# Output weights split on GpSimd alone, rows loaded ahead, and the decays' operations moved two steps behind their loads

## The chip, the cores and the metric

The kernel runs on one core of a Trainium2 chip. A core has a matrix engine (TensorE, PE in the profile), a vector engine (VectorE, DVE), an engine for functions of one input (ScalarE, ACT), a general one (GpSimd, POOL) and a sync engine whose queue issues most transfers (SyncE, SP). Each engine takes its instructions in the order in which they stand in its own queue; engines wait for each other through semaphores. The metric is the device time of one launch, in microseconds; the median over several runs is compared.

## The reference, cut to what matters

One layer of a streaming encoder runs for two groups of requests: a prompt of 2048 tokens and 8 streams with 16 new tokens each, 2176 tokens in all, 17 tiles of 128. A shared projection feeds two halves, a Mamba-2 state space mixer (SSD) and an attention with forget gates (FoX). Their results, concatenated, go through one output projection.

```python
def trunk(x, ...):
    n = rmsnorm(x, norm1_g[l])
    z, xbc, dt_raw, q, k, v, f_raw = split_columns(n @ w_in[l])
    y_ssd, ... = ssd_mixer(z, xbc, dt_raw, ...)
    y_fox = fox_prompt(q, k, v, logf)        # or fox_sample with the cache
    h = x + jnp.concatenate([y_ssd, y_fox], axis=-1) @ w_out[l]
    y_ffn, fc_new = conv_ffn(rmsnorm(h, norm2_g[l]), ...)
    x = h + y_ffn

def ssd_scan(xs, dt, a, bm, cm, s0):
    ...
    seg = a_cs[:, :, :, None, :] - a_cs[:, :, None, :, :]
    decay = jnp.exp(jnp.where(causal, seg, -jnp.inf))
    scores = jnp.einsum('bclhn,bcshn->bclsh', cc, bc) * decay
    y_diag = jnp.einsum('bclsh,bcshp->bclhp', scores, xdt)
    ...
```

## The kernel before

Tokens are worked in tiles of 128; the prompt's 16 tiles are numbered 0 to 15, the tile of the 8 streams is `SMP` (16). The prompt is also cut into four parts of 512 tokens. Up to about 1540 us the kernel interleaves three kinds of work on TensorE, and the order of TensorE's queue is written out by hand; behind that come the up- and down-projections (FFN). The order on the other engines and on SP's queue is set by a scheduler, which starts from program order and moves an instruction ahead or back by its own estimate of when its inputs are ready.

- **Attention** (`attention`, 320 steps). A step of `t_phase` computes one block of scores (`s<-q,k`, L728 and L729), its exponential on ScalarE (`pr<-s`, L733, kept in the list `exps`), and, two steps later, the product with the values (`pv<-pr,v`, L696). Beside it `s_phase` computes the maxima for a later head (`s<-ks,q`, L668; `nm`, L671). The tiles named `s` live in a PSUM pool of four buffers which attention and the state space chunks share, so TensorE can run only a few score blocks ahead of ScalarE's exponentials. Attention part p has 32(p+1) steps.
- **Side work** (`sides`). While a part of the attention runs, another generator is advanced in small units, evenly over the part's steps: the streams' attention in part 0, then the SSD chunks, one per tile (`ssd_chunk`). A chunk loads `xb` (convolved inputs, L525), `zt` (gate, L527) and `sg` (128x1024, the cumulated decays broadcast to all partitions, L529), each with one buffer. ScalarE turns `sg` into decays with eight Relu (L532, one per head) and one Exp over 1024 columns (L533). TensorE transposes and multiplies parts of `xb` (L536, L538), ScalarE copies one result to `bs` (L542), and further units use `sg` in the matmuls of L563, GpSimd's product `xe` (L557) in L573, and the state in L570. Every `yield` ends a unit, and the numbers in `sides` count them.
- **Fill** (`part_steps`, then `out_steps`): the input projections of the next part (`mm`, L397 to L399 and L444 to L446; `cmw` and `craw` are their weights) and, in the last part, the output projection. A tuple `("wait", n)` makes the fill pause for n attention steps.

`out_weights` prepares the output weights: eight tiles of 128x1024 are loaded (`raw`, two buffers, L896) and each is split into a rounded part and the rest (`wo`), because a product in full precision takes three matmuls of the fast type. ScalarE rounds (L109), GpSimd subtracts in two halves (L112), and `tc.issue_after(exps[-1])` keeps both behind the newest exponential. `out_proj(c)` loads the mixed rows of a tile (`raw<-mix_d`, L915, the same two buffers), splits them (`mx`, ScalarE L102 and VectorE L105), and runs 48 matmuls (`dn`, L923 to L925). Loads here stand on SP's queue. `load_v` clears half of a value tile on GpSimd (L636) before its load.

Of the kernel before, what the change touches and what calls it, by code (L numbers as in the profile page):

```python
# [11 lines left out]
AF = mybir.ActivationFunctionType  # L12
# [9 lines left out]
NB = 8  # L22
# [4 lines left out]
SMP = NTILE - 1  # L27
# [39 lines left out]
def hybrid_step(ctx: ExitStack, tc: tile.TileContext, i: dict, o: dict):  # L67
    nc = tc.nc
    V, S, G, T = nc.vector, nc.scalar, nc.gpsimd, nc.tensor
# [30 lines left out]
    def split(src, hi, lo, heng, leng):  # L100
        if heng is S:
            S.copy(hi, src)  # L102
        else:
            heng.tensor_copy(hi, src)
        leng.tensor_sub(lo, src, hi.bitcast(F32))  # L105

    def split2(src, hi, lo, leng):

        S.copy(hi, src)  # L109
        m = src.shape[1] // 2  # L110
        for c in (slice(0, m), slice(m, 2 * m)):
            leng.tensor_sub(lo[:, c], src[:, c], hi[:, c].bitcast(F32))  # L112
# [34 lines left out]
    def bt_(shape, tag, bufs, dt=F32):  # L147
        return bp.tile(shape, dt, tag=tag, name=tag, bufs=bufs)

    def pss():  # L150
        return psb.tile([P, 512], F32, tag="s", name="s", bufs=4)
# [370 lines left out]
    def ssd_chunk(c):  # L522
# [4 lines left out]
        dma(zt, z_d[c])  # L527
        sg = bt_([P, 8, P], "sg", 1)
        dma(sg.rearrange("p h l -> p (h l)"), ac_d[c:c + 1].rearrange("c h p -> c (h p)").to_broadcast([P, D]))  # L529

        for h in range(8):
            S.activation(sg[:, h], sg[:, h], AF.Relu, scale=-1.0, bias=acs[:, c, h:h + 1])  # L532
        S.activation(sg, sg, AF.Exp, scale=-1.0)  # L533
        pb = pss()
        for g in range(2):
            T.transpose(pb[:, g * P:(g + 1) * P], xb[:, 4 + g], ident)  # L536
# [156 lines left out]
    late, chores, exps = [], [], []  # L693
# [191 lines left out]


    tp = op = pso = None
    wo = []

    def out_weights():  # L890

        raws = {}

        def load(k):
            raws[k] = op.tile([P, D], F32, tag="raw", name="raw", bufs=2)
            dma(raws[k], i["w_out"][0, k * P:(k + 1) * P, :])  # L896

        load(0)
        load(1)
        yield ("wait", 3)  # L900
        for k in range(KT):
            w = op.tile([P, 2, D], F32R, tag="wo", name="wo", bufs=KT)
            with tc.issue_after(exps[-1]):
                split2(raws[k], w[:, 0], w[:, 1], G)
            wo.append(w)
            if k + 2 < KT:
                load(k + 2)
            yield ("wait", 2)

    def out_proj(c, after=None):  # L910
        mr = op.tile([P, KT, P], F32, tag="raw", name="raw", bufs=2)
        mx = op.tile([P, 2, KT, P], F32R, tag="mx", name="mx", bufs=2)

        for ks in ([slice(0, KT - 1), slice(KT - 1, KT)] if 12 <= c < 16 else [slice(0, KT)]):
            dA(mr[:, ks], mix_d[c][:, ks])  # L915
            split(mr[:, ks], mx[:, 0, ks], mx[:, 1, ks], S, V)
        y = op.tile([P, D], F32, tag="y", name="y", bufs=1)
        dA(y, i["xr"][c])
        ps = [pso.tile([P, 512], F32, tag="dn", name="dn") for _ in range(2)]

        def part(e, k):
            cc = slice(e * 512, (e + 1) * 512)
            T.matmul(ps[e], mx[:, 0, k], wo[k][:, 0, cc], start=k == 0, stop=False)  # L923
            T.matmul(ps[e], mx[:, 0, k], wo[k][:, 1, cc], start=False, stop=False)  # L924
            T.matmul(ps[e], mx[:, 1, k], wo[k][:, 0, cc], start=False, stop=k == KT - 1)  # L925

        with tc.issue_after(after) if after is not None else ExitStack():
            if c >= 12 and c != SMP:
                for k in range(KT):
                    for e in range(2):  # L930
                        part(e, k)
            else:
                for e in range(2):
                    for k in range(KT):
                        part(e, k)
                        if k % 2:
                            yield 1.36
        for e in range(2):
            cc = slice(e * 512, (e + 1) * 512)
            V.tensor_add(y[:, cc], y[:, cc], ps[e])  # L940
        dS(h_d[c], y)
# [190 lines left out]
    acs = cb.tile([P, NTILE, 8], F32, name="acs")  # L1132
# [31 lines left out]
    def chain(*gs):  # L1164
        for g in gs:
            yield from g

    def chunks(*cs):
        return chain(*(ssd_chunk(c) for c in cs))
# [28 lines left out]
    def out_steps():  # L1198
        A.close()
        open_out()  # L1200
        yield from out_weights()
        for c in [SMP] + list(range(11)):
            yield from out_proj(c)

    F = ExitStack()
    O = ExitStack()
# [1 line left out]
    def open_out():  # L1208
        nonlocal tp, op, pso
        tp = F.enter_context(tc.tile_pool(name="t3", bufs=2, reuse_waits="tile"))  # L1210
        op = O.enter_context(tc.tile_pool(name="op", bufs=1, reuse_waits="tile"))
        pso = O.enter_context(tc.tile_pool(name="pso", bufs=3, space=PSUM, reuse_waits="tile"))

    fill = [(0, 157.0, 20), (1, 140.0, 80), (2, 140.0, 172), (3, 69.0, 216), (4, 132.0, 318)]
    sides = {0: (sample_attention, 5 * NB + 1), 1: (lambda: chunks(SMP, 0, 1, 2), 49), 2: (lambda: chunks(3, 4, 5, 6, 7), 51),
             3: (lambda: chunks(*range(8, 16)), 81)}

    with tc.manual_schedule(engines={nc.tensor.engine}):
        bodies = [a_body(0)]
# [9 lines left out]
        n = hold = 0  # L1229
# [3 lines left out]
        for u in att:  # L1233
            if u is None:
                credit += 3.0
            else:
                if u != side_p:
                    for _ in side or ():
                        pass
                    side_p = u  # L1240
                    f, total = sides[u]
                    side, given, cnt = f(), 0, 0
                n += 1
                cnt += 1
                while given < total * cnt // (32 * (u + 1)):
                    next(side, None)
                    given += 1
                if hold:
                    hold -= 1
                    continue  # L1250
                if gen is not None:
                    start = fill[stage - 1][2] if stage else 0
                    credit += fill[stage][1] / (fill[stage][2] - start)
            while gen is not None and credit > 0 and not hold:
                c = next(gen, None)
                if c is None:
                    stage += 1
                    gen = (part_steps(stage) if stage < NPART else out_steps()) if stage < len(fill) else None
                elif isinstance(c, tuple):
                    hold = c[1]  # L1260
                else:
                    credit -= c
# [13 lines left out]
    for w, cs in zip(FPARTS[0], ((11, 12, 13), (14, 15))):  # L1276
        prep(w, True)
        for c in cs:

            for _ in out_proj(c, None if c >= 12 else pv_ins[-1]):  # L1280
                pass
# [109 lines left out]
```

## Time and profile before

| | us |
|---|---|
| median of 3 runs | 3158.28 (3156.93 to 3160.4) |
| the profiled execution's own time | 3159.18 |
| its span, from first to last instruction | 3157.5 |
| TensorE busy, with modelled ends | 3039.0 |
| VectorE, ScalarE, GpSimd busy | 1788.8, 1066.7, 865.8 |

Time lies in three stretches: up to about 460 us the first part's projections and the streams' attention, from 460 to 1540 us attention, chunks and fill together, and from there the FFN. What TensorE's idle time waited for stands behind an instruction in square brackets in the timeline: the idle time in us, and the releaser.

### The profile page before, as it was taken

The page shows a single profiled execution, that of the slowest core. Times are in us where ns is not written, and L with a number is a line of the kernel's source. Part 1 is how long each engine was busy: PE and PEld are TensorE (multiplying, and loading weights), DVE is VectorE, ACT ScalarE, POOL GpSimd, SP SyncE. Part 2 cuts the span into 40 slices and gives each one's busy share as a digit, 9 for nine tenths or more (in the row PEclk, how much of TensorE's full clock was granted, in tenths as well). Part 3 has the DMA queues.
Part 4 walks back from the last instruction along what each step waited for, and adds up shares of the span by engine and source line. Part 5 has one row for each costly group of instructions (what it writes and reads, how often), then busy time and mean ns, then how long its engine had stood idle before and what let it go on. Part 6 is the DMA issues. An engine that isn't in the chain of part 4 may idle for free.

```text
span 3157.5 us, 45849 instructions
## 1 busy us (share of the span) xinstructions
PE 3039.0 (96%) x17888; PEld 2682.1 (85%) x17888; DVE 1788.8 (57%) x3294; ACT 1066.7 (34%) x1927; POOL 865.8 (27%) x654
## 2 busy tenths in 40 slices
PE   7988998899999998999999999999999999999998
PEld 7886877787788775777899999999999999999998
DVE  4264466647565654543455555566555556766666
ACT  3343344444444444332322232233222223332322
POOL 3322322222222212000233232333223232433332
PEclk9998999899999999999999999999999999999999
DMA  4856675575556546445522121232121122322221
GB/s 123 247 174 202 200 244 158 181 223 165 162 155 204 153 132 187 161 148 181 171 67 67 54 69 61 72 116 79 61 67 61 60 67 83 105 67 81 74 69 65
DMA packets 233137, 395.77 MB, mean 125 GB/s; under 512 B 62544, under 2 KB 118488, under 8 KB 232920
## 3 DMA queue, kind: packets, MB, share of 16 engines
q1 hardware_dynamic: 181224, 238.41, 24.3%
q10 hardware_dynamic: 51696, 154.43, 15.8%
q8 instruction: 141, 2.31, 0.3%
q14 instruction: 76, 0.62, 0.1%
HBM read 314.51 MB, written 78.25 MB: 124 GB/s over the span
## 4 chain that ended last, share of the span: by engine, by line
PE 85%; DMA 8%; DVE 2%; ACT 2%; issue 1%; SPq 1%; POOL 1%; ACTq 0%; DVEq 0%; POOLq 0%
PE mm L120 11%; PE mm L121 11%; PE mm L122 11%; PE pv L696 6%; PE dn L1025 5%; PE dn L1026 5%; PE dn L1027 5%; PE mm L444 3%; PE mm L445 3%; PE mm L446 3%; DMA xt<-in_xr 2%; PE dn L923 2%; PE dn L925 2%; PE dn L924 2%; PE mm L397 2%; PE mm L399 2%
## 5 line engine op out<-in xcount | busy, mean ns | idle before, releaser
L105 POOL TENSOR_TENSOR wr<-raw,wr 128x1024 fp32r<-128x1024 f32 x198 | 476.5, 2415 | 1032.5 <-ACT wr L102 1024.5
L120 PE MATMUL mm<-nT,wr 128*128 128x386 f32 (+1 forms) x2112 | 696.4, 330 | 1.3 <-ACT wr L102 0.8
L121 PE MATMUL mm<-nT,wr 128*128 128x386 f32 (+1 forms) x2112 | 695.3, 329 | 0.1
L122 PE MATMUL mm<-nT,wr 128*128 128x386 f32 (+1 forms) x2112 | 694.4, 329 | 0.0
L1003 DVE SCALAR_TENSOR_TENSOR ac<-mm,cw,ac 128x384 f32<-128x384 f32 (+1 forms) x528 | 301.6, 571 | 344.8 <-ACT ac L1001 337.1
L1001 ACT ACTIVATE ac<-mm,cw 128x384 f32<-128x384 f32 (+1 forms) x264 | 172.7, 654 | 784.6 <-PE mm L122 784.0
L1028 DVE TENSOR_TENSOR y<-y,dn 128x512 f32<-128x512 f32 x374 | 255.0, 684 | 267.4 <-PE dn L1027 264.6
L121 PEld LDWEIGHTS mm<-nT,wr 128*128 128x128 f32 x2112 | 399.3, 189 | 6.8 <-DVE nT L105 0.3
L120 PEld LDWEIGHTS mm<-nT,wr 128*128 128x128 f32 x2112 | 397.5, 188 | 7.7 <-ACT wr L102 1.1
L122 PEld LDWEIGHTS mm<-nT,wr 128*128 128x128 f32 x2112 | 397.9, 188 | 5.7
L112 POOL TENSOR_TENSOR cmw<-craw,cmw 128x512 fp32r<-128x512 f32 (+1 forms) x192 | 248.6, 1317 | 467.8 <-ACT cmw L109 348.1
L444 PE MATMUL mm<-nT,cmw 128*128 128x256 f32 (+2 forms) x1024 | 309.7, 302 | 12.7 <-DVE cac L489 8.6
L671 DVE TENSOR_REDUCE nm<-s 128x1 f32<-128x512 f32 (+2 forms) x320 | 192.9, 607 | 198.6 <-PE s L668 114.1
L445 PE MATMUL mm<-nT,cmw 128*128 128x256 f32 (+2 forms) x1024 | 299.0, 292 | 0.0
L446 PE MATMUL mm<-nT,cmw 128*128 128x256 f32 (+2 forms) x1024 | 299.0, 292 | 0.0
L1025 PE MATMUL dn<-wr,ht 128*128 128x512 f32 x748 | 294.4, 394 | 2.9 <-DVE y L1028 1.7
L696 PE MATMUL pv<-pr,v 128*128 128x512 f32 (+3 forms) x640 | 293.5, 549 | 0.5 <-issue 0.5
L1026 PE MATMUL dn<-wr,ht 128*128 128x512 f32 x748 | 292.7, 391 | 0.0
L1027 PE MATMUL dn<-wr,ht 128*128 128x512 f32 x748 | 290.1, 391 | 0.0
L102 ACT CAST wr<-raw 128x1024 fp32r<-128x1024 f32 x198 | 203.2, 1042 | 174.1 <-PE dn L1027 161.4
L733 ACT ACTIVATE pr<-s 128x512 f32<-128x512 f32 (+1 forms) x320 | 169.3, 531 | 237.3 <-PE s L729 173.2
L668 PE MATMUL s<-ks,q 68*128 68x512 f32 (+2 forms) x320 | 199.8, 630 | 20.0 <-ACT pr L733 11.2
(294 smaller groups left out, 5174.9 us busy)
## 6 DMA issues: line engine op xcount, KB each, us to landing
raw<-in_w_up ACTq DMA_DIRECT2D x132, 512.0 KB
raw<-in_w_down ACTq DMA_DIRECT2D x66, 512.0 KB
craw<-in_w_cm ACTq DMA_DIRECT2D x64, 512.0 KB
k<-k_d SPq DMA_DIRECT2D x80, 256.0 KB
craw<-in_w_tm ACTq DMA_DIRECT2D x24, 512.0 KB
q_d<-qk SPq DMA_DIRECT2D x96, 128.0 KB
k_d<-qk SPq DMA_DIRECT2D x96, 128.0 KB
ks<-k_d SPq DMA_DIRECT2D x80, 136.0 KB
```

What stands on the lines that cost most here:

```text
L105: leng.tensor_sub(lo, src, hi.bitcast(F32))
L120: T.matmul(ps[:, :W], whi(k), wt[:, 0, k, :W], start=k == 0, stop=False)
L121: T.matmul(ps[:, :W], whi(k), wt[:, 1, k, :W], start=False, stop=False)
L122: T.matmul(ps[:, :W], wlo(k), wt[:, 0, k, :W], start=False, stop=k == n - 1)
L444: T.matmul(ps[:, :W], wc[:, 0, k, :], wk[:, 0], start=k == 0, stop=False)
L445: T.matmul(ps[:, :W], wc[:, 0, k, :], wk[:, 1], start=False, stop=False)
L446: T.matmul(ps[:, :W], wc[:, 1, k, :], wk[:, 0], start=False, stop=k == KT - 1)
L696: m = T.matmul(pv[:, of:512], vr[:, jj], pr[:, :512 - of], start=first, stop=last)
L1003: V.scalar_tensor_tensor(ac[:, 0:n], ps[:, j:j + n], cw2[:, ct, j:j + 1], ac[:, 0:n], op0=ALU.mult, op1=ALU.add)
L1025: T.matmul(ps, ht[:, 0, ts_], wd[:, 0, cc], start=x == 0, stop=False)
L1026: T.matmul(ps, ht[:, 0, ts_], wd[:, 1, cc], start=False, stop=False)
L1027: T.matmul(ps, ht[:, 1, ts_], wd[:, 0, cc], start=False, stop=x == len(g) - 1)
```

## The change

- `ssd_chunk`: two more `yield` stand between the three loads and the operations on them, and Relu and Exp on `sg` must stand behind the newest exponential of the attention.
- `out_weights`: GpSimd does both halves of the split, the rounding copy and one subtraction over 1024 columns; ScalarE has no part in it, and nothing ties it to an exponential.
- `out_proj`: the load and the split of a tile's rows are a function of their own, `out_rows`, called for the next tile when the first half of the current tile's matmuls is written.
- `sides`: part 1 has the chunks SMP, 0, 1 (before also 2), part 2 has 2 to 6 (before 3 to 7), part 3 has 7 to 15 (before 8 to 15); the counts of units follow the new yields.

Lines in and behind `ssd_chunk` are numbered three higher in the changed kernel (L532 is L535), and those of `out_proj` seven or nine higher.

```diff
@@ ssd_chunk
         dma(sg.rearrange("p h l -> p (h l)"), ac_d[c:c + 1]...)
-        for h in range(8):
-            S.activation(sg[:, h], sg[:, h], AF.Relu, scale=-1.0, bias=acs[:, c, h:h + 1])
-        S.activation(sg, sg, AF.Exp, scale=-1.0)
+        yield
+        yield
+        with tc.issue_after(exps[-1]):
+            for h in range(8):
+                S.activation(sg[:, h], sg[:, h], AF.Relu, scale=-1.0, bias=acs[:, c, h:h + 1])
+            S.activation(sg, sg, AF.Exp, scale=-1.0)
@@ out_weights
             w = op.tile([P, 2, D], F32R, tag="wo", name="wo", bufs=KT)
-            with tc.issue_after(exps[-1]):
-                split2(raws[k], w[:, 0], w[:, 1], G)
+            split(raws[k], w[:, 0], w[:, 1], G, G)
@@ out_proj
-    def out_proj(c, after=None):
+    def out_rows(c):
         mr = op.tile([P, KT, P], F32, tag="raw", name="raw", bufs=2)
         mx = op.tile([P, 2, KT, P], F32R, tag="mx", name="mx", bufs=2)
         for ks in (...):
             dA(mr[:, ks], mix_d[c][:, ks])
             split(mr[:, ks], mx[:, 0, ks], mx[:, 1, ks], S, V)
+        return mx
+    def out_proj(c, after=None, mx=None, nxt=None):
+        if mx is None:
+            mx = out_rows(c)
...
                         if k % 2:
                             yield 1.36
+                    if e == 0 and nxt is not None:
+                        ready.append(out_rows(nxt))
@@ out_steps
-        for c in [SMP] + list(range(11)):
-            yield from out_proj(c)
+        cs = [SMP] + list(range(11))
+        mx = out_rows(cs[0])
+        for n, c in enumerate(cs):
+            yield from out_proj(c, None, mx, cs[n + 1] if n + 1 < len(cs) else None)
+            mx = ready.pop() if ready else None
@@ sides
-    1: (lambda: chunks(SMP, 0, 1, 2), 49), 2: (lambda: chunks(3, 4, 5, 6, 7), 51),
-    3: (lambda: chunks(*range(8, 16)), 81)
+    1: (lambda: chunks(SMP, 0, 1), 45), 2: (lambda: chunks(2, 3, 4, 5, 6), 61),
+    3: (lambda: chunks(*range(7, 16)), 109)
```

The next two extracts are ScalarE's queue around the decays of one chunk late in attention part 2, before and then after. `sg` is the decays' tile, `pr` an exponential of the attention, `cac` and `cth` belong to the convolution, `cmw` and `craw` to projection weights.

```order
L733 ACTIVATE pr_11170<-s_11166 128x256
L487 ACTIVATE cac_11207<-mm_11153,cw1_169 128x256
L109 CAST cmw_11499<-craw_11497 128x1024
L532 ACTIVATE sg_11612<-sg_11612,acs_185 128x128 x7
L733 ACTIVATE pr_11240<-s_11236 128x128
L532 ACTIVATE sg_11612<-sg_11612,acs_185 128x128
L497 ACTIVATE cth_11208<-cac_11207 128x256
L533 ACTIVATE sg_11612<-sg_11612 128x1024
```

```order
L736 ACTIVATE pr_11612<-s_11608 128x128
L535 ACTIVATE sg_11534<-sg_11534,acs_185 128x128 x8
L387 DMA craw_12130<-in_w_tm 128x4x256
L545 COPY bs_11666<-s_11630 128x256
L536 ACTIVATE sg_11534<-sg_11534 128x1024
L497 ACTIVATE cth_11549<-cac_11548 128x256
L736 ACTIVATE pr_11657<-s_11654 128x512
```

The load of a chunk's `sg` waits on SP until the chunk before has used the buffer (L563). Counted in attention steps on TensorE, between that use and the last exponential ahead of the first Relu, there are 0 to 2 steps in all 16 chunks but the first before, and 8 to 21 after (11 in the chunk shown). The Exp (L536) and the copy `bs` now stand in one row with the Relu, with no exponential of the attention between them.

The next two are GpSimd's queue in the second half of the output weights' split, before and after. `raw` is a loaded tile, `wo` its two parts, `v` a value tile that is cleared before its load, `xe` a chunk's product.

```order
L112 TENSOR_TENSOR wo_13122<-raw_13005,wo_13122 128x512 x2
L636 MEMSET v_13362 128x4x64
L112 TENSOR_TENSOR wo_13178<-raw_13051,wo_13178 128x512 x2
L557 TENSOR_TENSOR xe_13176<-xd_13172,te_186 128x512
L112 TENSOR_TENSOR wo_13235<-raw_13126,wo_13235 128x512 x2
```

```order
L104 CAST wo_12995<-raw_12878 128x1024
L104 CAST wo_13051<-raw_12943 128x1024
L105 TENSOR_TENSOR wo_12995<-raw_12878,wo_12995 128x1024
L639 MEMSET v_13088 128x4x64
L105 TENSOR_TENSOR wo_13051<-raw_12943,wo_13051 128x1024
L639 MEMSET v_13152 128x4x64
L104 CAST wo_13120<-raw_12998 128x1024
L560 TENSOR_TENSOR xe_13040<-xd_13036,te_186 128x512
L104 CAST wo_13169<-raw_13054 128x1024
L105 TENSOR_TENSOR wo_13120<-raw_12998,wo_13120 128x1024
```

The casts are new on GpSimd and go in pairs ahead of the subtractions: two casts, then two subtractions. A cast waits for a load, and the product `xe` now stands behind the cast of the seventh tile.

The last extract is SP's queue at the end of that stage, after. `raw_13229` and `raw_13262` receive the rows of the first two tiles, SMP and 0.

```order
L626 DMA k12_13519<-k1_d_59 128x512
L627 DMA k12_13519<-k2_d_60 68x512
L917 DMA raw_13229<-mix_d_64 128x1024
L632 DMA ks_13427<-k2_d_60 68x512
L917 DMA raw_13262<-mix_d_64 128x1024
```

The rows' loads wait there for GpSimd (their buffers are the weights' last two) and stand behind the load of the key block `k12_13519`, which waits for TensorE to have finished the block four before it (there are four buffers). On ScalarE the casts of both tiles' rows stand ahead of the next exponential with only a copy between them; before, two exponentials stood between them.

More of the change, by code (lines that the diff above doesn't have):

```diff
@@ L887, in hybrid_step @@
     tp = op = pso = None
-    wo = []
+    wo, ready = [], []
     def out_weights():
@@ L1214, in hybrid_step @@
     fill = [(0, 157.0, 20), (1, 140.0, 80), (2, 140.0, 172), (3, 69.0, 216), (4, 132.0, 318)]
-    sides = {0: (sample_attention, 5 * NB + 1), 1: (lambda: chunks(SMP, 0, 1, 2), 49), 2: (lambda: chunks(3, 4, 5, 6, 7), 51),
-             3: (lambda: chunks(*range(8, 16)), 81)}
+    sides = {0: (sample_attention, 5 * NB + 1), 1: (lambda: chunks(SMP, 0, 1), 45), 2: (lambda: chunks(2, 3, 4, 5, 6), 61),
+             3: (lambda: chunks(*range(7, 16)), 109)}
     with tc.manual_schedule(engines={nc.tensor.engine}):
```

## The prediction

> **What bounds the kernel now.** I read the chain that ended last on the page, then the busy time by stretches, then the timeline of TensorE for its idle times, and last ScalarE's timeline in front of those.
>
> ```profile
> PE 85%; DMA 8%; DVE 2%; ACT 2%; issue 1%; SPq 1%; POOL 1%; ACTq 0%; DVEq 0%; POOLq 0%
> ...
> 760.00:1160.00 400.00, 389.75 (x2543) 315.88 (x2542) 237.06 (x455) 175.50 (x370) 102.10 (x110) 0.99 0.54 161
> 1160.00:1244.00 84.00, 66.09 (x321) 43.88 (x320) 42.81 (x66) 38.12 (x73) 25.53 (x28) 0.90 0.64 189
> 1244.00:1540.00 296.00, 295.66 (x1384) 222.87 (x1383) 132.27 (x209) 91.63 (x189) 18.25 (x42) 1.00 0.49 164
> ```
>
> The first row is the chain by engine: TensorE carries 85% of it, so only its idle time, and time at a lower clock, can be won. In the rows by stretch the second number is the stretch's length, the third TensorE's busy time, and the third from the end the granted clock. The output weights' stretch (1160 to 1244) lacks 17.9 of 84 us. Behind it TensorE is full. Its idle times from 460 us on that the change can reach:
>
> ```profile
> 476.49 0.58 PE L444 MATMUL mm<-nT,cmw 128*128 128x260 f32 x1 [4.96 <-DVE cac L489]
> 503.68 1.13 PE L588 MATMUL s<-k,cm 128*128 128x256 f32 x4 [1.41 <-ACT pr L733]
> 557.13 2.07 PE L588 MATMUL s<-k,cm 128*128 128x256 f32 x4 [7.85 <-DVE ss L198]
> 616.65 0.38 PE L668 MATMUL s<-ks,q 68*128 68x256 f32 x1 [1.68 <-ACT pr L733]
> 787.65 0.50 PE L668 MATMUL s<-ks,q 68*128 68x512 f32 x1 [1.74 <-ACT pr L733]
> 858.96 0.50 PE L729 MATMUL s<-q,k 68*128 68x512 f32 x1 [2.43 <-DVE q L686]
> 909.80 0.33 PE L728 MATMUL s<-q,k 128*128 128x128 f32 x1 [1.38 <-ACT pr L733]
> 1036.18 1.13 PE L570 MATMUL s<-sst,xb 128*128 128x256 f32 x4 [3.55 <-ACT pr L733]
> 1182.02 0.80 PE L668 MATMUL s<-ks,q 68*128 68x512 f32 x1 [5.07 <-ACT pr L733]
> 1202.57 0.50 PE L728 MATMUL s<-q,k 128*128 128x512 f32 x1 [2.12 <-ACT pr L733]
> 1238.16 2.08 PE L570 MATMUL s<-sst,xb 128*128 128x256 f32 x4 [9.06 <-ACT pr L733]
> ```
>
> Most wait for an exponential (L733). An exponential costs half a microsecond; what was late is what stood before it in ScalarE's queue. There the decays sit, waiting for their own load:
>
> ```profile
> 614.26 0.40 ACT L532 ACTIVATE sg<-sg,acs 128x128 f32<-128x128 f32 x1 [4.33 <-DMA sg<-ac_d]
> 721.88 2.45 ACT L532 ACTIVATE sg<-sg,acs 128x128 f32<-128x128 f32 x8 [2.43 <-DMA sg<-ac_d]
> 784.78 2.45 ACT L532 ACTIVATE sg<-sg,acs 128x128 f32<-128x128 f32 x8 [3.77 <-DMA sg<-ac_d]
> 1033.81 2.15 ACT L532 ACTIVATE sg<-sg,acs 128x128 f32<-128x128 f32 x7 [5.71 <-DMA sg<-ac_d]
> ...
> 1024.97 8.82 DMA sg<-ac_d
> ...
> 1187.98 0.23 PE s L728
> 1189.54 0.24 PE s L728
> ```
>
> The row at 1024.97, from the chain, is the load: issued at 1024.97, landed 8.82 us later, while ScalarE had reached the Relu at 1028.1 (1033.81 less 5.71). From there to the next exponential ScalarE gave TensorE nothing for 7.9 us, of which TensorE bridged 4.3 and stood 3.55. At 784.78 the hole is 3.77 and 2.45, 6.2 us, less 1.74 leaves 4.5 bridged. So TensorE bears a hole of about 4.4 us; at 721.88 one of at least 4.9 cost nothing.
>
> Each longer stop also costs clock:
>
> ```profile
> 476.00:482.00 6.00, 5.42 (x24) 4.78 (x25) 5.77 (x12) 3.35 (x8) 3.81 (x3) 0.59 0.12 31
> 616.00:622.00 6.00, 5.34 (x32) 5.31 (x32) 2.25 (x13) 5.91 (x15) 2.38 (x2) 0.72 0.32 103
> 788.00:794.00 6.00, 6.00 (x30) 5.15 (x29) 3.41 (x6) 4.66 (x12) 2.63 (x3) 0.72 0.17 52
> 858.00:864.00 6.00, 5.04 (x14) 2.81 (x15) 4.16 (x8) 1.39 (x3) 0.28 (x1) 0.72 0.95 301
> 1036.00:1042.00 6.00, 5.82 (x26) 5.24 (x27) 4.69 (x9) 2.88 (x7) 0.00 (x0) 0.72 0.60 195
> ```
>
> Busy time times what is missing to 1.00 is lost: 2.2, 1.5, 1.7, 1.4 and 1.6 us. [...]
>
> **The decays, two units later.** No operation is added. Between the buffer's release and the Relu's place stood 0 to 2 attention steps and now stand 8 to 21. ScalarE reached the Relu of the load above 3.1 us after its issue; the shortest attention steps take 1.56 us (the two L728 rows), and eight of them, 12.5 us, cover 8.82. So the six stops that a waiting Relu caused go: 4.96, 1.41, 1.68, 1.74, 1.38 and 3.55, 14.7 us (the one at 1202.57 is counted with the output weights), and with four of them the clock's 2.2, 1.5, 1.7 and 1.6, 7.0 us. What is late next is the block of decays itself, which no exponential divides any more:
>
> ```profile
> L533 ACT ACTIVATE sg<-sg 128x1024 f32<-128x1024 f32 x17 | 17.9, 1052 | 0.2
> L542 ACT COPY bs<-s 128x256 f32<-128x256 f32 x17 | 6.3, 373 | 1.1 <-PE s L538 0.2
> L710 ACT COPY rdb<-pv 64x512 f32<-64x512 f32 x32 | 18.6, 581 | 0.5
> L109 ACT CAST cmw<-craw 128x1024 fp32r<-128x1024 f32 x88 | 91.5, 1040 | 15.9 <-PE mm L399 15.9
> ```
>
> Eight Relu 2.45, `bs` 0.37 and Exp 1.05 make a hole of 3.9 us, under the 4.4. In six chunks the queue adds the two copies at a head's end (0.58 each) or a weight cast (1.04): holes of 4.9 to 6.5 us, 5.4 us beyond the bearable in all, 6.9 with the clock after the longest. Projection matmuls covered such a hole at 721.88; I take 3 us of cost between 0 and 7.
>
> `xb` is loaded two units ahead too. The stop at 858.96 (2.43 us and 1.4 of clock) lies on a chain that began with an `xb` load but went through VectorE's other work; I take half, 1.9 us, between 0 and 3.8.
>
> **The output weights.** ScalarE loses eight casts of 1.04 us, GpSimd gains them; its subtractions are as many elements as before. The chain there is one of loads: two buffers, the next load starts when a subtraction ends.
>
> ```profile
> 1170.48 9.86 DMA raw<-in_w_out
> 1213.15 7.96 DMA raw<-in_w_out
> 1224.79 11.76 DMA raw<-mix_d
> 1243.69 0.28 PE dn L923
> ...
> 844.30 4.31 DMA xb<-xb_d
> ...
> L105 POOL TENSOR_TENSOR wr<-raw,wr 128x1024 fp32r<-128x1024 f32 x198 | 476.5, 2415 | 1032.5 <-ACT wr L102 1024.5 <-PE dn L1026 4.4 <-PE tp L979 3.7
> L557 POOL TENSOR_TENSOR xe<-xd,te 128x512 f32<-128x512 f32 x17 | 17.7, 1044 | 44.1 <-DVE xd L553 44.0
> L636 POOL MEMSET v<- 128x256 f32 x80 | 24.9, 313 | 336.9 <-PE pv L696 259.3 <-issue 67.2 <-DMA h_d<-y 5.9
> masks.py:197 POOL MEMSET ident<- 128x128 f32 x1 | 0.2, 206 | 0.3 <-POOLq L1380 0.3
> ```
>
> Before, the first weight load is issued at 1170.48 and the first output matmul starts at 1243.69: 73.2 us. No row shows a cast on GpSimd. The two clears differ by 107 ns for 128 columns, so 1024 written columns take 0.96 us; the two-input row sets the other end, 2.4. A cast has one input, so I take 1.0, nearer to the clear. [...] With load time L and cast c, the new chain is: first load 9.86; two casts and a subtraction, 2c + 2.4; two rounds of a load, a cast, two subtractions and small work (0.6), each L + c + 5.4; a subtraction and a clear, 2.7; the eighth load, its cast and two subtractions, L + c + 5.1; then the rows of tile 0, issue 0.3, L, and two casts and an exponential on ScalarE, 2.7, since the exponential behind both casts frees the PSUM buffer that TensorE needs. The sum is 34.0 + 5c + 4L. With c = 1.0 and L = 7.96, the one weight load that the chain shows inside the stage, it is 70.9, so 2.3 us are won. With the shortest load of this size, 4.31, it is 56.2 (17 won); with the longest, 11.76, and c = 2.4 it is 93.0 (20 lost). I take the gain of 2.3.
>
> Behind the waiting casts on GpSimd stand the clears of `v` and the product `xe`; SP's key and value loads queue behind weight loads that wait for GpSimd. Those delay TensorE inside the stage, but it must reach the first output matmul anyway, and that matmul hangs on the chain above.
>
> **The rows ahead, and the chunks.** The rows' load and split cost nothing and gain nothing: from 1244 to 1540 TensorE is busy 295.66 of 296 us whatever ScalarE waits for; without that cover a tile would wait for a load, up to 11.76. Chunks 2 and 7 each pass to the next attention part: the same matmuls elsewhere, zero. The stop at 557.13 (7.85 us) is VectorE's crowd of the streams' chunk and the next part's norm; fewer units per step there could thin it or shift it: zero, between a gain of 10 and a loss of 5.
>
> **Sum.** The execution's own time 3159.18 - 14.7 - 7.0 + 3.0 - 1.9 - 2.3 = 3136.3; its median stands 0.9 lower, so 3135.4.
>
> **Rivals.**
> - *The weights' chain is longer.* ScalarE and GpSimd no longer overlap: two casts, then two subtractions, with only two buffers. With L = 11.76 and c = 1.0 the stage takes 86.0, 15.1 more than forecast: 3150.5. For it speaks the row of 11.76; against, that it shared the engines with other transfers that now also wait.
> - *The weights' chain is shorter.* While SP's queue stands, a load has the transfers to itself; L = 5.5 gives 61.0: 3125.5.
> - *The stops move and do not go.* ScalarE's load gone, VectorE is next (2.43 at 858.96, 7.85 at 557.13 are its). If half of the 21.7 comes back as such waits and the blocks cost 7, the time is 3150.3; if all comes back, 3157. Against it: most stops name ScalarE with the load behind it.
> - *Slower: the undivided block of decays.* If TensorE bears not 4.4 but 2.4 us (attention steps without projection matmuls beside them), a block of 3.9 us costs 1.5 and, with the clock, 3 us in each of 17 chunks: 51 us less the 3 counted, 3183. It turns slower than 3164.6 from some 1.9 us a chunk. Against it speak 784.78, 721.88 and the full stretch from 1244.
>
> **Chances.** Forecast 0.52 (own range 3126 to 3147), shorter chain 0.14, longer chain 0.14 (half of it still over 0.2% faster), stops that move 0.12 (mostly within 0.2%), slower 0.08. 0.2%, some 6 us, is about what a measurement of this kernel can tell from no change. Faster 0.75, same 0.17, slower 0.08. The range, 3118 to 3156, reaches into the shorter chain and the stops that move and leaves some 0.15 out.
>
> **What would show it.** Right: no Relu row on ScalarE waits for `sg<-ac_d` by more than 1 us; TensorE's idle time in the stretch that was 760 to 1160 falls from 10 to under 4 us; the first weight load to the first `dn` takes 65 to 77 us. Wrong: stops that name L733 right behind a block of Relu, Exp and `bs`; GpSimd casts of over 2 us; a stage of over 85 us; VectorE named for new stops before 760.

## The result, and the profile after

The changed kernel takes 3140.02 us (median of 4 runs, 3138.48 to 3144.17) beside 3158.66 for the kernel before: a ratio of 0.9946, 95% interval 0.9933 to 0.9958. The forecast was 3135.4, and the time lies inside its range. The profiled execution took 3140.58 us. The experiments will show that the total is a gain of some 28 us less 9 to 10 us of costs that the forecast had at zero or at a small gain, and that the gain has another cause than the forecast gave.

The page's span, its chain by engine, and two of the stretches shown before:

```profile
span 3138.8 us, 45833 instructions
PE 60%; DMA 1%; DVE 1%; ACT 0%; POOL 0%; issue 0%; SPq 0%; DVEq 0%; POOLq 0%; ACTq 0%
760.00:1160.00 400.00, 396.18 (x2616) 319.23 (x2614) 242.85 (x462) 178.33 (x378) 103.21 (x111) 1.00 0.56 169
1160.00:1244.00 84.00, 68.96 (x284) 47.11 (x285) 42.94 (x59) 27.39 (x59) 29.67 (x27) 0.90 0.54 170
```

The row of the chain can't be set beside the 85% from before: this time the chain was followed back only to 1160.71 us, and its shares add up to 62%, about the time behind that point.

Between 760 and 1160 us TensorE's idle time fell from 10.3 to 3.8 us, and the granted clock rose from 0.99 to 1.00. The stretch of the output weights is little better than it was: 15.0 of 84 us idle for 17.9, at the same clock of 0.90.

To see where the time went I use three landmarks, matmuls that stand behind the same projection and attention work in both programs: a projection matmul that waits for `g_2k` while attention part 1 runs, a score block in part 2 that waits for `q` (858.96 in the prediction's list), and a matmul at the start of the FFN. In the timeline of TensorE, number in front the time in us, before:

```profile
637.90 0.38 PE L444 MATMUL mm<-nT,cmw 128*128 128x256 f32 x1 [0.48 <-DVE g_2k L331]
1555.79 0.44 PE L120 MATMUL mm<-nT,wr 128*128 128x386 f32 x1 [0.78 <-ACT wr L102]
```

and after, with the idle times of 0.8 us and more from 460 us on, beside the landmarks:

```profile
478.86 0.50 PE L671 MATMUL s<-ks,q 68*128 68x512 f32 x1 [3.58 <-ACT pr L736]
539.10 1.13 PE L591 MATMUL s<-k,cm 128*128 128x256 f32 x4 [2.42 <-DVE cm L585]
548.74 0.77 PE L731 MATMUL s<-q,k 128*128 128x512 f32 x1 [3.27 <-DMA k<-k_d]
550.50 0.79 PE L732 MATMUL s<-q,k 68*128 68x512 f32 x1 [1.00 <-DMA k<-k_d]
563.49 0.47 PE L731 MATMUL s<-q,k 128*128 128x512 f32 x1 [1.61 <-DMA k<-k_d]
565.43 0.80 PE L732 MATMUL s<-q,k 68*128 68x512 f32 x1 [1.46 <-DMA k<-k_d]
626.95 0.39 PE L444 MATMUL mm<-nT,cmw 128*128 128x256 f32 x1 [0.33 <-DVE g_2k L331]
842.18 0.50 PE L732 MATMUL s<-q,k 68*128 68x512 f32 x1 [0.81 <-DVE q L689]
1162.19 1.57 PE L576 MATMUL s<-xe,bs 128*128 128x256 f32 x4 [2.92 <-POOL xe L560]
1178.90 1.09 PE L616 MATMUL s<-ident,yt 128*128 128x128 f32 x4 [6.01 <-DVE yt L612]
1190.57 0.51 PE L732 MATMUL s<-q,k 68*128 68x512 f32 x1 [1.10 <-DVE q L689]
1209.48 0.74 PE L616 MATMUL s<-ident,yt 128*128 128x128 f32 x4 [1.30 <-DVE yt L612]
1215.60 0.51 PE L671 MATMUL s<-ks,q 68*128 68x512 f32 x1 [2.42 <-ACT zt L617]
1218.17 0.69 PE L539 MATMUL s<-ident,xb 128*128 128x128 f32 x2 [2.00 <-ACT pr L736]
1537.84 0.45 PE L120 MATMUL mm<-nT,wr 128*128 128x386 f32 x1 [0.77 <-ACT wr L102]
```

The FFN starts 18.0 us earlier and behind it nothing changed (1601.7 us to the end of the span before, 1601.0 now). 11.0 us were won up to the first landmark, 5.8 from there to the second (858.96 before, 842.18 now), and 1.2 in the last stretch. One chunk less runs in the first stretch and one more in the last; a chunk's matmuls take 5.7 us, so without that shift the first stretch won some 5 us and the last some 7. Two of the six stops of the forecast, 4.9 us, had stood in the last stretch and are gone. In the stretch of the output weights the stops have other names now and nearly as many microseconds: those of 0.3 us and more between 1130 and 1310 us add up to 17.1, for 17.7 before.

What ScalarE waited for in front of its Relu is told by the view of one source line, before and after (count, shortest, median and longest in ns; then the idle time by releaser):

```profile
L532 ACT ACTIVATE sg<-sg,acs x136: 384/387/404, 472.6 to 1401.2; 128x128 f32<-128x128 f32 x136
...
  DMA sg<-ac_d: 35.0, 14
```

```profile
L535 ACT ACTIVATE sg<-sg,acs x136: 386/391/403, 478.7 to 1413.7; 128x128 f32<-128x128 f32 x136
```

35.0 us in 14 waits for the decays' loads before, beside two waits of other names, 10.4 us together; after, the view lists no idle time at all.

### The profile page after: what moved, and what is told of

Read it like the earlier page. It is cut to its first block, busy times and chain, and to the rows that moved or that the text cites. A ratio compares the mean times of both kernels' runs of the same rounds, so it can differ in the third digit from the quotient of the medians.

```text
span 3138.8 us, 45833 instructions
## 1 busy us (share of the span) xinstructions
PE 3035.6 (97%) x17888; PEld 2680.5 (85%) x17888; DVE 1789.7 (57%) x3294; ACT 1057.5 (34%) x1919; POOL 871.8 (28%) x654
## 4 chain that ended last, share of the span: by engine, by line
PE 60%; DMA 1%; DVE 1%; ACT 0%; POOL 0%; issue 0%; SPq 0%; DVEq 0%; POOLq 0%; ACTq 0%
PE mm L120 11%; PE mm L121 11%; PE mm L122 11%; PE dn L1034 5%; PE dn L1035 5%; PE dn L1036 5%; PE dn L930 2%; PE dn L932 2%; PE dn L931 2%; PE pv L699 2%; PE s L732 1%; PE s L731 1%; PE s L671 0%; PE tp L988 0%; DMA raw<-mix_d 0%; PE s L576 0%
## 5 line engine op out<-in xcount | busy, mean ns | idle before, releaser
L121 PE MATMUL mm<-nT,wr 128*128 128x386 f32 (+1 forms) x2112 | 695.7, 329 | 0.1
```

Of the source, the lines that this page charges most:

```text
L121: T.matmul(ps[:, :W], whi(k), wt[:, 1, k, :W], start=False, stop=False)
```

## Experiment: one part of the change at a time

Four kernels, each the kernel before with one part of the change. The kernel before took 3159.74 us beside them.

Decays alone:

```diff
+        yield
+        yield
+        with tc.issue_after(exps[-1]):
             for h in range(8): S.activation(sg[:, h], ..., AF.Relu, ...)
             S.activation(sg, sg, AF.Exp, scale=-1.0)
-    1: SMP, 0, 1, 2: 49    2: 3 to 7: 51    3: 8 to 15: 81
+    1: SMP, 0, 1, 2: 57    2: 3 to 7: 61    3: 8 to 15: 97
```

> The kernel before with the move of the decays' operations alone (two units behind their loads, tied to the last exponential of a block); the chunks stay with the parts that had them, and the counts of units grow to 57, 61 and 97. Theory one, all that was gained is the loads that Relu no longer waits for: as fast as the kernel after, 3140 us with 4 to spare, and no stop of ScalarE on sg<-ac_d. Theory two, a share of 6 to 10 us of the gain comes from ScalarE, which no longer casts the output weights: 3147 to 3150 us. Theory three, a like share comes from the new distribution of the chunks: 3148 us or more.

Measured: 3131.39 us, ratio 0.9907 (0.9894 to 0.9920). Faster by 28.4, and 8.6 below the whole change. None of the three theories had that: the rest of the change costs time.

Output weights alone (`split(raws[k], w[:, 0], w[:, 1], G, G)` in place of `split2` behind the exponential):

> The kernel before with GpSimd casting and subtracting the output weights alone, nothing else. Theory one (the gain is the decays' loads): 3158 us with 3 to spare, as before; the stage from the first weight load to the first matmul of the output stays at 70 to 77 us, against 73.2 before. Theory two: 6 to 10 us faster, 3148 to 3152 us.

Measured: 3169.2 us, ratio 1.0027 (1.0017 to 1.0037): slower by 9.5. Not all of it is shown to come from the edit: its profiled execution (3169.16) is 7.5 us behind the kernel before already at the first landmark (645.43 for 637.90), though up to there the order on every engine is the same. From the second landmark to the FFN, where the edit is, it loses some 4 us. Rows ahead alone:

> The kernel before with the rows of the output loaded half a tile ahead, nothing else. Theory one: 3158 us with 2 to spare. Theory two (a part of the gain is in the output's stage): 2 to 4 us faster.

Measured: 3162.52 us, ratio 1.0007 (0.9996 to 1.0017): no difference that can be told. Chunks alone:

> The kernel before with the new distribution of the chunks alone (two, five and nine of them to the three parts besides the sample's, counts 39, 51 and 91). Theory one: 3158 us with 3 to spare, and the stops of ScalarE on the decays' loads are all there, though not at the same times. Theory three: 6 to 12 us faster, 3146 to 3152 us, by fewer units beside the streams' part.

Measured: 3171.34 us, ratio 1.0036 (1.0024 to 1.0048): slower by 11.6; between the first two landmarks it takes 234.5 us for 221.1. Theories two and three had the sign wrong, and theory one was too low for the decays and blind to these two costs.

Why do the weights and the chunks cost time when they stand alone? The same view of the Relu line, for the weights alone and then for the chunks alone:

```profile
  DMA sg<-ac_d: 56.9, 16
```

```profile
  DMA sg<-ac_d: 55.1, 15
```

ScalarE's waits for the decays' loads rose from 35.0 to 56.9 and 55.1 us. Two places show it, ScalarE and TensorE with the weights alone, then with the chunks alone:

```profile
1205.18 1.86 ACT L532 ACTIVATE sg<-sg,acs 128x128 f32<-128x128 f32 x6 [10.90 <-DMA sg<-ac_d]
1207.58 2.08 PE L696 MATMUL pv<-pr,v 128*128 128x512 f32 x2 [7.40 <-ACT pr L733]
1243.06 2.44 ACT L532 ACTIVATE sg<-sg,acs 128x128 f32<-128x128 f32 x8 [8.73 <-DMA sg<-ac_d]
1250.98 0.79 PE L922 MATMUL dn<-wo,mx 128*128 128x512 f32 x1 [12.84 <-ACT mx L102]
```

```profile
723.42 2.44 ACT L532 ACTIVATE sg<-sg,acs 128x128 f32<-128x128 f32 x8 [9.41 <-DMA sg<-ac_d]
726.83 2.04 PE L573 MATMUL s<-xe,bs 128*128 128x256 f32 x4 [8.28 <-ACT pr L733]
```

In these kernels the Relu stand at worse places. The wait that the move of the decays takes away is also the one by which the other two are seen to hurt, so the four results do not add up: the sum of the four differences is 4.5 us of gain, and the whole change gained 18.6.

## Experiment: the two halves of the decays' move

The move has two halves: two more units between loads and operations, and a tie that keeps Relu and Exp behind the newest exponential. Each alone, on the kernel before (3161.12 us beside them).

```diff
 units only                                   tie only
+        yield                               +        with tc.issue_after(exps[-1]):
+        yield                                            Relu x8, Exp
```

> The kernel before with the two units between a chunk's loads and its operations, but without the tie of Relu and Exp to the newest exponential (counts 57, 61 and 97, old chunks, nothing else of the change). Theory one, as the prediction has it (what counts is that the load is long landed when ScalarE reaches the Relu): 3131 us with 4 to spare, as the whole of the decays' move. Rival, the tie counts (it keeps the block of decays from standing ahead of an exponential that is due): 3140 to 3150 us.

Measured: 3148.95 us, ratio 0.9967 (0.9954 to 0.9981).

> The kernel before with the tie of Relu and Exp to the newest exponential, but without the two units between loads and operations (counts 49, 51 and 81). Theory one: the Relu still reach ScalarE's turn while their load is on its way, and the time stays at 3158 us with 4 to spare. Rival, the tie counts: 3140 to 3150 us.

Measured: 3140.24 us, ratio 0.9942 (0.9928 to 0.9956). The tie alone wins 20.9 us, the two units alone 12.2: both expectations of theory one, and with them the forecast's reason, fell. The largest row of the Relu line's waits with the units alone, then the only one with the tie alone:

```profile
  DMA sg<-ac_d: 39.5, 15
```

```profile
  DMA k<-in_s0T: 6.0, 1
```

With the units alone, 39.5 us of waits for the load stay; with the tie alone, that row is gone. The one that is left belongs to the first chunk, whose Relu ScalarE still reaches 0.2 us behind the issue of its load; the view names another load for it. One chunk each, the load's issue on SP's queue and the Relu on ScalarE, units alone and then tie alone:

```profile
1086.67 0.33 SPq L529 DMA_DIRECT2D sg<-ac_d  x1
1092.48 1.86 ACT L535 ACTIVATE sg<-sg,acs 128x128 f32<-128x128 f32 x6 [3.12 <-DMA sg<-ac_d]
```

```profile
1079.96 0.34 SPq L529 DMA_DIRECT2D sg<-ac_d  x1
1107.29 2.44 ACT L533 ACTIVATE sg<-sg,acs 128x128 f32<-128x128 f32 x8
```

Over the 17 chunks ScalarE was at the Relu 2.7 us after the load's issue in the kernel before (median), and 2.7 us with the units alone, with one exponential between; with the tie alone it was 26.1 us, with eight between. The two units moved the Relu in the program, and the scheduler put it right behind the load again. The tie takes that freedom away.

What the two units win is not in the sum of these waits. They add some 8 us to the tie (28.4 won for 20.9, in two sets of runs) and 12.2 alone. TensorE's stops of 0.3 us and more between 460 and 1310 us are 46.6 us before, 35.1 with the units alone, 33.0 with the tie alone and 26.1 with both, so the gain is in stops. With the units alone, two waits are shorter at places that had stops (3.09 us at 905.7 before, 1.66 now; 5.71 at 1033.81, 1.79 now), but the stop of 1.74 us is gone too though the Relu of that chunk still waits 4.01 us, at 785.9. So a waiting Relu need not cost TensorE anything. Why the units make it cheaper was not taken apart and stays open.

## Experiment: what takes the 9 us back

Two theories were left for the kernel after: A, GpSimd's split of the weights; B, the chunk that passes to part 3. Beside these four the kernel before took 3158.74.

```diff
 after, old split of the weights      after, old chunks
-    split(raws[k], ..., G, G)       -    SMP,0,1: 45   2..6: 61   7..15: 109
+    with tc.issue_after(exps[-1]):  +    SMP,0,1,2: 57 3..7: 61   8..15: 97
+        split2(raws[k], ..., G)
```

> The kernel after with the old split of the output weights (ScalarE casts, GpSimd subtracts in halves, behind the newest exponential), all else as after. The decays' move alone reached 3131, some 9 us under the kernel after, so something in the other parts takes 9 us back. Theory A, it is the split on GpSimd: 3131 us with 3 to spare, and the stage from the first weight load to the first output matmul 62 to 66 us. Theory B, it is the chunk that passes from attention part 1 to part 3: 3140 us with 3 to spare, as the kernel after.

Measured: 3137.2 us, ratio 0.9928 (0.9915 to 0.9940). The interval overlaps that of the kernel after; its stage is 70.6 us (1148.8 to 1219.4), not the 62 to 66 of theory A.

> The kernel after with the old distribution of the chunks (SMP, 0, 1, 2; 3 to 7; 8 to 15; counts 57, 61, 97), all else as after, so the decays' move with the new split and the rows ahead. Theory A (the split on GpSimd takes the 9 us): 3140 us with 3 to spare. Theory B (the chunk that passes from part 1 to part 3 takes them): 3131 us with 3 to spare. Half and half would be 3135.

Measured: 3132.97 us, ratio 0.9911 (0.9898 to 0.9924), apart from the 0.9933 to 0.9958 of the kernel after. Theory B: the new distribution costs 7 us here, with no wait for a decays' load in play. It differs from the decays alone by weights and rows, and by only 1.6 us, within the intervals. Its stage is 62.3 us (1153.45 to 1215.72) with GpSimd's split, and that of the decays alone 62.4 (1146.95 to 1209.37) with the old one: with the tie and the old chunks the stage is 11 us shorter than the 73.2 of the kernel before, whichever engine casts.

The kernel after with GpSimd's work in another order:

```diff
+    with tc.issue_after(subs[-1]) if subs else ExitStack():
         G.tensor_copy(w[:, 0], raws[k])
+    subs.append(G.tensor_sub(w[:, 1], raws[k], w[:, 0]...).ins)
```

> The kernel after with one order more on GpSimd: the cast of weight tile k+1 stands behind the subtraction of tile k, so that a subtraction never waits for the next tile's load, and each raw buffer is given back as soon as its tile is done. If theory A holds by that mechanism (in the kernel after casts come in pairs, and the rows of the first tile are loaded only when the subtraction of tile 6 has stood behind the cast of tile 7): the stage shrinks from 73.5 to 63 to 67 us and the time to 3133 us with 4 to spare. If the split costs for another reason (the length of the loads), or the chunk costs (theory B): 3140 us with 3 to spare.

Measured: 3133.18 us, ratio 0.9912 (0.9898 to 0.9926). The time is as expected, the stage is not: 70.6 us (1144.0 to 1214.6). The landmarks warn against the total: at the second one the profiled execution is 2.0 us ahead of the kernel after (840.19 for 842.18), though nothing was changed up to there, and 4.5 us are won from there to the FFN, where the change is. So I count 4 to 5 us for the order, not 7.

The chunks the other way, on the decays alone (SMP, 0 to 3: 69; 4 to 8: 61; 9 to 15: 85):

> The kernel before with the decays' move, and the chunks shifted to the other side: SMP, 0 to 3 in part 1, 4 to 8 in part 2, 9 to 15 in part 3 (counts 69, 61, 85). A chunk's matmuls take 5.7 us by the lines of the kernel before. Theory B (part 1 is not filled by TensorE, part 3 is, so a chunk is free in the one and paid in the other): 4 to 10 us faster than the decays' move alone, 3121 to 3127 us. If a chunk costs the same everywhere: 3131 us with 3 to spare.

Measured: 3128.54 us, ratio 0.9900 (0.9887 to 0.9914), not to be told from the decays alone. Its first landmark comes 5.5 us later (632.66 for 627.20), about the chunk's 5.7 us of matmuls; and the kernel after with the old chunks comes there 6.7 us later than the kernel after (633.60 for 626.95). Executions of programs that are the same up to there differ by 2.0 us in one pair and 7.5 in another, so this is no proof; but both differences have the size of a chunk, and the whole time shows no gain either. So theory B's reason, that part 1 has room, is not borne out; a chunk's matmuls are no cheaper there, and they are not what the move costs.

What it costs can be seen in stops: from the second landmark to the FFN the kernel after takes 14.2 us more than with the old chunks (695.7 for 681.5), of which 5.7 are the chunk's matmuls. TensorE's stops between 1130 and 1310 us make up 6.5 of the rest (17.1 for 10.6), and the clock over 1130 to 1300 is 0.95 for 0.96. In the chain of waits of the kernel after one such stop reads:

```profile
1165.43 6.60 DMA raw<-in_w_out
...
1172.17 1.04 POOL wo L104
1173.21 2.30 POOL wo L105
1175.51 0.66 POOL ss L116
1176.20 2.56 DVE yt L612
1178.76 0.14 issue
1178.90 1.09 PE s L616 x4
```

A chunk's normalisation (`ss`, 0.66 us) stood on GpSimd behind a cast that waited for its weight load and behind a subtraction; VectorE's `yt` waited for it, and TensorE stood 6.01 us for the transposes of `yt`. It is the pattern of the Relu, on another queue: work that is due stands behind work that waits for a transfer. That a chunk more in this part brings such a pair under the weights more often fits this row, but was not tested by itself. The 2.56 us of `yt` are part of it; the last section comes back to them.

## Experiment: all together

```diff
 weights tile by tile, and chunks           the run beside it
+    SMP,0..3: 69  4..8: 61  9..15: 85     +    SMP,0..3: 69  4..10: 85  11..15: 61
```

> The kernel after with GpSimd's weights tile by tile and the chunks shifted the other way (SMP, 0 to 3; 4 to 8; 9 to 15; counts 69, 61, 85). The tile order gave 7 us, the earlier chunks some 3 beside the decays' move alone and the moved chunk of the kernel after cost 7. If what the moved chunk costs is crowding in the output weights' stage (more units for each attention step there): TensorE's stops between 1140 and 1300 us fall from 16.8 us in the kernel after to under 8, and the time is 3125 us with 4 to spare. If these gains are the same microseconds, won twice: 3130 us with 3 to spare.

Measured: 3139.11 us, ratio 0.9935 (0.9919 to 0.9950). Both expectations missed. The stops between 1130 and 1310 us grew to 21.4 us; the largest, with ScalarE and VectorE in front of it:

```profile
1214.64 1.04 ACT L102 CAST mx<-raw 128x1024 fp32r<-128x1024 f32 x1 [9.00 <-DMA raw<-mix_d]
1215.71 1.23 DVE L105 TENSOR_TENSOR mx<-raw,mx 128x1024 fp32r<-128x1024 f32 x1 [8.95 <-ACT mx L102]
1216.86 0.87 DVE L612 SCALAR_TENSOR_TENSOR yt<-yt,ss,ngB 128x256 f32<-128x256 f32 x2
1217.48 1.09 PE L616 MATMUL s<-ident,yt 128*128 128x128 f32 x4 [11.45 <-DVE yt L612]
```

The same pattern a third time: `yt` stood on VectorE behind the split of the first rows, which waited through ScalarE for the load of the rows. The kernel after has a smaller one of this kind: ScalarE's cast of the rows waited for their load, and the stops of 2.42 and 2.00 us (1215.60 and 1218.17) came from the copy `zt` and the exponentials behind it.

```profile
1214.01 1.04 ACT L102 CAST mx<-raw 128x1024 fp32r<-128x1024 f32 x1 [6.18 <-DMA raw<-mix_d]
```

> As the run beside it (weights tile by tile), but with two more chunks moved from part 3 to part 2 (SMP, 0 to 3; 4 to 10; 11 to 15; counts 69, 85, 61), so that beside the output weights' stage fewer units run for each attention step, and more in part 2. If crowding in that stage is what costs: its stops fall below 5 us, and the time is 3 to 6 us under the run beside it, unless part 2, where TensorE stood under 2 us in all, pays it back. If only the number of a chunk's matmuls counts: the same as the run beside it, with 3 to spare.

Measured: 3136.61 us, ratio 0.9926 (0.9912 to 0.9940). The stops between 1130 and 1310 us fell from 21.4 to 12.3 us, not below 5, and those between 700 and 1130 rose from 1.8 to 5.3; a stop of 8.73 us of the same kind (`yt`) stands at 1205.00. The intervals of the two times overlap, so thinning the units is not shown to help. The number of units beside the stage does not set its price alone. Which instruction stands behind a waiting one counts too: the run with the tiles in order changed that alone, and its stops there are 13.7 us for the 17.1 of the kernel after.

The best kernels are the decays alone (3131.39) and the same with earlier chunks (3128.54); both intervals lie below that of the whole change.

## Why the prediction was right, and where its steps were not

- **The decays: 20.6 us forecast, 28.4 measured alone.** That six stops come from a Relu waiting for its load, and that they would go, was right: five (1.41, 1.68, 1.74, 1.38 and 3.55 us) went, and no wait for a Relu took their place. But that a Relu's wait costs by its length is not shown, as the run with the units alone says. The step "eight of them, 12.5 us, cover 8.82" took the right order from the changed program but gave it to the two units; they alone leave 39.5 us of waits, the tie alone none. The term was also too small: between 1130 and 1310 us, in the stage of the output weights, which the forecast counted apart, the decays alone leave 11.7 us of stops of the 17.7 before. Only 2.12 of these (1202.57) had stood behind a Relu; why the others shrank was not taken apart.
- **The stop of 4.96 us** did not go; 3.58 of it came back at 478.86, at a clock of 0.72 in the 6 us behind it. It was not a plain case of the Relu either: with the tie alone a stop of 5.21 us stands there (474.18). In the kernel after, ScalarE waits there for a store:

```profile
477.45 0.42 ACT L497 ACTIVATE cth<-cac 128x256 f32<-128x256 f32 x1 [4.52 <-DMA xb_d<-cth]
```

- **The undivided block** was put at 3 us. Between 480 and 1160 us no stop of the kernel after above 0.7 us names ScalarE, and the slower rival that rested on it did not come: idle time from 760 to 1160 fell under the 4 us that the forecast set. Its cost lies nearer to zero.
- **The stop at 858.96**, half of 3.8 us: with the one in front of it 3.36 us became 1.42. The term was right, without the clock.
- **The output weights, 2.3 us won:** alone they lost 9.5, some 4 of it seen where the edit is, through the Relu's waits; with the tie in place they cost between nothing and 3 (1.6 by one pair of kernels, 2.8 by another, neither outside the intervals). The stage is 73.5 us (1145.95 to 1219.4) for 70.9 forecast. That they are near is luck: the same split has a stage of 62.3 us with the old chunks, and the sum for the stage has no term for the chunks or the tie. The cast's price, the unknown of that step, was right: 1.0 forecast, and the view of its line has

```profile
L104 POOL CAST wo<-raw x8: 1036/1037/1195, 1155.9 to 1201.2; 128x1024 fp32r<-128x1024 f32 x8
```

  The step that failed is "Those delay TensorE inside the stage, but it must reach the first output matmul anyway": the stage's length is not the cost; the stops of `xe` (2.92 us) and `yt` (6.01) are time in which no chunk or attention matmul ran. The forecast also gave the split nothing for what it took off ScalarE. Before, the stops of 5.07 and 9.06 us (1182.02 and 1238.16) stood behind exponentials that came after ScalarE's casts of the weights, the second also after a cast of rows:

```profile
1180.42 1.04 ACT L109 CAST wo<-raw 128x1024 fp32r<-128x1024 f32 x1 [5.79 <-DMA raw<-in_w_out]
1230.82 1.04 ACT L109 CAST wo<-raw 128x1024 fp32r<-128x1024 f32 x1 [6.43 <-DMA raw<-in_w_out]
```

  With the old split, all else as after, stops of 4.41, 2.49 and 4.22 us name ScalarE there; with the new one, GpSimd's `xe` and `yt` stand in their place. So the split moved such stops from one queue to another.
- **The chunks, zero:** 7 us lost in the kernel after, 11.6 alone, outside the -10 to +5 that the forecast allowed. It asked what the matmuls cost and what VectorE's crowd at 557.13 would do, not what would then stand behind a waiting instruction: in the weights' stage in the kernel after, behind the Relu when the chunks move alone (8.28 us at 726.83). The crowd was put at zero rightly: 7.85 and 2.20 us there became 9.8 in five stops (VectorE named for new stops before 760 was a sign set for the waits moving; the one at 539.10 stayed the only one of its kind).
- **The sum** was 4.6 us from the result, because a gain 8 us too small and costs of 9 to 10 us, which it had at a small gain, nearly cancelled. That the total came out near is luck.

## What to carry to other kernels

Where a scheduler sets the order, moving an operation in the source need not move it, if the scheduler's estimate brings it back: read the order on the engine after the edit, and where it must hold, tie it. When pricing an edit, do not stop at the operation's own wait: list what stands behind each instruction that waits for a transfer, on every in-order queue, since most of the large stops that were followed here came from there. And parts that each change an order do not add up: test each alone, and again beside the others.

## What the runs showed of the hardware that I had not expected

Two stops of like length had different prices. Granted clock is the third number from the end; the kernel after around its stop of 2.42 us at 539.10, then the kernel before around its stop of 1.74 us at 787.65:

```profile
539.00:541.00 2.00, 1.90 (x9) 1.70 (x10) 2.00 (x4) 0.00 (x0) 1.22 (x1) 1.00 0.35 134
541.00:543.00 2.00, 2.00 (x13) 1.39 (x11) 2.00 (x5) 1.47 (x5) 0.00 (x0) 1.00 0.78 207
```

```profile
787.00:789.00 2.00, 1.35 (x6) 1.30 (x7) 0.69 (x1) 1.99 (x5) 0.00 (x0) 0.77 0.08 33
789.00:791.00 2.00, 2.00 (x12) 2.00 (x11) 0.72 (x2) 1.97 (x3) 0.00 (x0) 0.50 0.00 0
```

The longer stop left the clock at 1.00, the shorter was followed by 0.50. In the kernel before, the stop of 2.12 us at 1202.57 was followed by 1.00 too (1202 to 1208). The forecast's "each longer stop also costs clock" fits the five stops it lists, with 0.59 to 0.72 around and behind them, but not all. So the length of one stop does not decide alone; what does, no run here tells apart.

The second thing is VectorE beside GpSimd. In the kernels before and after, `yt` of the normalisation (128x256, L609 and L612) runs 68 times. Six of these began while GpSimd was at a subtraction of 1.27 to 2.36 us; they took 1.45 to 2.55 us and ended 0.3 us behind it. The other 62 took 0.47 to 0.49 us. The one of 2.55, at 1176.20 in the kernel after, began 0.07 us into a subtraction of an output weight (2.34 us) and is some 2 of the 6.01 us that TensorE then stood. The changed kernel subtracts 1024 columns of an output weight at once (2.34 us in this one), the kernel before 512 (1.27 and 1.44 us in the two beside which `yt` took 1.45 and 1.48), so it may hold VectorE up for longer. That the subtraction is what holds `yt` up is read from these times; no run changed it alone.
